# A two-layer decode and prefill step on one core: weight sums go along the mixer, norm-finishing products come later in TensorE's queue, GpSimd makes a part of the low parts at the token join

## The chip, the core and the metric

The kernel runs on one core of a Trainium2 chip. The metric is the device time of one execution, in microseconds (us), as the median of several. The engines are TensorE (PE in the rows; PEld is its weight load), VectorE (DVE), ScalarE (ACT), GpSimd (POOL) and SyncE (SP); SP issues most of the DMAs, GpSimd some. `SPq` and `POOLq` are what an engine's queue issues without computing.

## The reference, cut to what matters

Two layers run over 1,088 tokens (1,024 of a prompt, 64 of a sample: 8 sequences of 8). Layer 0 mixes by an RWKV-7 recurrence of 12 heads, layer 1 by latent attention of 6 heads over a shared latent (for the sample over a paged cache of 4,096 tokens); both add a memory attention. Behind each mixer come the output projection and a gated convolutional feed-forward block:

```python
x = x + jnp.concatenate([o_tok, o_mem], axis=-1) @ P['w_o'][l]           # 1024 x 1024
f, c = conv_glu(rms_norm(x, P['norm_ffn'][l]), conv0[l], P['w_ffn_up'][l],
                P['conv_w'][l], P['conv_b'][l], P['w_ffn_down'][l])
x = x + f
# conv_glu: u = xn @ w_up (1024 x 5632); gate, val = u[..., :2816], u[..., 2816:]
#           h = silu(conv3(gate)) * val;  return h @ w_down (2816 x 1024), ...
# rms_norm: x * rsqrt(mean(x * x) + eps) * gain
```

All is float32. An exact product of two float32 operands is made as three TensorE products of a high part and a low part (L481 to L483 and L1354 to L1356): `high` is the operand rounded by ScalarE (L210, L1137, L1313), `low` is operand minus high, a subtraction by VectorE or GpSimd (L211, L1138, L1314).

## The kernel before, in words

The tokens stand in two halves of 544, each of two quarters of 272. The stages follow one another in the trace: the mixer of layer 0 (up to 790 us its units, up to 940 us what ends it), the output projection of layer 0 (940 to 1130 us), its feed-forward block (to 1840 us), the start of layer 1 with the latents (to 1968 us), its prompt attention (1968 to about 2450 us), the decode over the paged cache (to about 2650 us), the output projection of layer 1 (to 2775 us), its feed-forward block and the final norm (to 3541 us).

**Weight sums.** The up-projection saves products: `combine_x` (L1214 on) makes seven combinations of a half's activations, and each 128 columns take seven combinations of the weights. Four of those are sums of blocks of `w_ffn_up`, called vg, gg, vgg and all, and `sum_weights(l)` (L1277 on) has them made in DRAM by DMAs alone, 32 per layer, 1,408 KB each, all on L1292. Sixteen are plain moves, issued by SP on the queue that also loads every weight tile. Sixteen are moves that add to what is there, issued by GpSimd. They come in the order: move vg, move gg, add vg, add gg, move vgg, add vgg, move all, add all, four row blocks `r` of each. A vgg or an all move waits for an add, and its add waits for that move; each is kept where the program puts it in its queue. `sum_weights` is a generator, and one `yield` is one DMA.

**Order of the work.** The order is written by hand: `merge` takes a list of generators with weights and steps them in proportion. The mixer has 12 units (6 head pairs by 2 halves), and `s.take(sums, 4)` lets each unit from the second on issue four steps of layer 0's sums; they are used up in the eighth. Layer 1's sums go two at a time into `prompt_attention`, one pair per iteration.

**Norm finishing.** The squares of a residual go through ScalarE (L1174) and are added up by GpSimd into `acc` (L1175). `scales` (L1203 on) then sums over the partitions by a TensorE product with a constant (L1209) and makes the reciprocal root by ScalarE (L1211, L1212). TensorE takes its instructions in order, so it stands at L1209 until GpSimd's last addition. In `trunk_tail`, `project(h)` ends with the `scales` of its half. `squares(0)` (L1177 on; L1187, L1188) makes the same for the first half behind the feed-forward block of layer 0, for the latents, in `down_last`.

**Join.** A feed-forward block runs five groups of columns for the first half, then five for the second: `ups` and `down` of the group before are merged. Where the halves join, `combine_x(1)` (VectorE L1224, GpSimd L1227 to L1230, 28 splits by ScalarE and VectorE at L1137 and L1138) runs beside `down(0, 4)`, whose weights are split too (L210, L211).

Of the kernel before, what the change touches and what calls it, by code (L numbers as in the profile page):

```python
# [9 lines left out]
F32 = mybir.dt.float32  # L10
# [4 lines left out]
ALU = mybir.AluOpType  # L15
# [71 lines left out]
HT = NT // 2  # L87
QT = NT // 4
G4 = [(QT * i, QT) for i in range(4)]
# [11 lines left out]
class Step:  # L101
# [171 lines left out]
    def mixer_a(s, od, qmd, kvd):  # L273
# [95 lines left out]
        mkv = s.memory_kv(kvd, 0, ("tp", "ch", "y"))  # L369
        sums = s.sum_weights(0)  # L370
        for i in range(nu):
            g = []
            if i == 1:
                for j in range(1, (len(s.prows) + 127) // 128):
                    s.load_params(j, [nc.sync])
            if i > 1:
                g.append((chain(units[i - 2]), s.PW[0] + s.PW[1] * units[i - 2][0], s.PW[2]))
            if i:
                u = units[i - 1]
                g.append((s.a_inner(u[1], u[0], ctx[u]), s.PW[3] + s.PW[4] * u[0], s.PW[5]))  # L380
            g.append((front(units[i]), 130 if units[i][1] else 220))
            if i == 0:
                g.append((mkv, 22))
            else:
                g.append((s.take(sums, 4), 4))
            s.merge(g)
# [747 lines left out]

    def split(s, hi, lo, x):
        nc = s.nc
        nc.scalar.copy(hi, x)  # L1137
        nc.vector.tensor_tensor(lo, x, hi.bitcast(F32), ALU.subtract)  # L1138

# [37 lines left out]
    def squares(s, h, acc):  # L1177

        nc = s.nc
        for d in range(KC):  # L1180
            for c0, a in acc.items():
                xv = s.x[:, d, c0:c0 + QT]
                if d == 0:
                    nc.scalar.activation(a, xv, AF.Square)
                else:
                    sq = s.st([128, QT], "nt", s.ntb)
                    nc.scalar.activation(sq, xv, AF.Square)  # L1187
                    nc.gpsimd.tensor_tensor(a, a, sq, ALU.add)  # L1188
            yield
        for c0 in acc:  # L1190
            s.scales((c0, QT), acc)

    def new_acc(s, h, tag="acc", n=HT):

        a = s.st([128, n], tag, 2 if tag == "acc" else 1)
        s.rstd[h] = s.t(s.xp, [128, HT], "rstd", 2)
        return {QT * (2 * h + i): a[:, QT * i:QT * i + QT] for i in range(2)}
# [16 lines left out]
    def combine_x(s, h, gain, xs):  # L1214


        nc = s.nc
        xs += [s.new_xq() for _ in range(7)]
        lo, hi = slice(0, QT), slice(QT, HT)
        for j in range(4):  # L1220
# [10 lines left out]
            src = (a[0][:, lo], t[1], t[0], t[2], t[3], a[1][:, hi], a[1][:, lo])  # L1231
            for (xh, xl), z in zip(xs, src):
                s.split(xh[:, j], xl[:, j], z)
                yield
# [81 lines left out]

    def ffn(s, l, xs0, after, pre=None):

# [95 lines left out]
        groups = [(0, 4), (4, 4), (8, 4), (12, 5), (17, 5)]  # L1414
        hs = {}
        operands = [xs0, []]

        def ups(h, i):
            c0, n = groups[i]
            hs[h, i] = []  # L1420
            if h and i == 0:
                yield from s.combine_x(1, ("norm_ffn", 8 * l), operands[1])
            for c in range(c0, c0 + n):
                yield from up(h, c, operands[h], hs[h, i])

# [6 lines left out]

        def down(h, i):
            yield from s.gemm_x(lambda d: wd(i, d), quarters(hs.pop((h, i))), h)

        def down_last():
# [25 lines left out]
            first = s.seq(*[after(g, None) for g in G4[:2]])  # L1462
            if l == 0:
                first = s.seq(s.squares(0, s.new_acc(0, "cv", EW)), first)
            return (yield from s.gemm_t(ws, hs.pop((1, i)), acc, after, [[first, s.conv_out(l, cout)], []]))
# [41 lines left out]
    def trunk_tail(s, l, od, xd, qmd, xst):  # L1507

        nc, I = s.nc, s.I
        with s.phase(f"f{l}", {"mm": 6, "dn": 2}):  # L1510
            s.xp = s.sp
            s.ntb, s.LAG, s.WA = 6, 2, 8
            xdv = xd.rearrange("(k p) t -> p k t", p=128)
# [6 lines left out]
            with s.sub(f"o{l}"):  # L1520
                first = [s.x_tile(i, nc.gpsimd) for i in range(2)] if l == 0 else []
                s.lay(([128, QT], "nt", s.ntb), ([128, HT], "tw", 2), ([128, HT], "acc", 2))
                os_ = []
# [28 lines left out]

                def project(h):
                    acc = s.new_acc(h)
                    yield from s.gemm_x(w, os_[h], h, acc, "mm")
                    for g in G4[2 * h:2 * h + 2]:
                        s.scales(g, acc)
                    yield

# [4 lines left out]
                if l == 0:  # L1564
                    s.drain(s.load_x(first))
                s.merge([(project(0), 17), (parts(os_[1]), 16)])
                s.merge([(project(1), 17), (s.combine_x(0, ("norm_ffn", 8 * l), xs), 32)])
            xl = {}

# [6 lines left out]
            with s.sub(f"n{l}"):  # L1576
                pend = s.emit(s.ffn(l, xs, stored if l == 0 else s.final, s.first_latent if l == 0 else None))
                if l:
                    s.drain(pend)
# [344 lines left out]
    def prompt_attention(s, od):  # L1924
        s.AT = (3, 2, 1, 2, 6, 3)
        s.HN = ((8, 12, 12, 1000), (8, 12, 14, 1000))
        with s.phase("pa", dict(zip(("sc", "tp", "o", "mm"), s.AT))):
# [7 lines left out]
            pr = None  # L1935
            sums = s.sum_weights(1)
            for i in range(len(us) + 1):
# [6 lines left out]
                if i < len(us):  # L1944
# [6 lines left out]
                    if pr is not None:  # L1951
                        k = s.HN[h % 2][Q]
                        g.append((s.take(pr, k), min(k, 40)))
                s.merge([(ao, n), (s.take(sums, 2), 2)] + g)

# [468 lines left out]
```

## Time and profile before

| | |
|---|---|
| median of 3 runs | 3540.04 us (3537.58 to 3558.76) |
| the profiled execution's own time | 3542.77 us |
| its span, first to last instruction | 3541.0 us |
| mean granted TensorE clock | 0.953 of full speed |
| PE busy | 3283.3 us, 93% |
| DVE, ACT, POOL busy | 2331.1, 1724.7, 811.9 us |

TensorE is busy for 93% of the span, so the reader looks for the stretches where it is not, or where its clock is low, and for what ended each wait. A wait row reads: engine, tile and line that waited, what came last, microseconds in total, how often, the longest. A timeline row has start, duration, engine, line, operation, tiles, and in brackets the idle time before it and what ended it.

### The profile page before, as it was taken

The numbers are of one execution on the slowest core, as the hardware profiler recorded it, in microseconds if no ns is written. First come the engines' busy times: TensorE is split into PE (matmuls) and PEld (weight loads), VectorE is DVE, ScalarE is ACT, GpSimd is POOL, SyncE is SP. The second block draws the span as 40 slices with busy tenths as digits, with TensorE's granted clock in tenths as the row PEclk, the third lists the DMA queues.
The fourth block names the chain that finished last, engine by engine and source line by source line (L and its number), as shares of the span: only waits on it lengthen the run. The fifth ranks groups of instructions, "written<-read, shape, count | busy, mean of one in ns | idle before, by whom it ended". The sixth has DMA issues, their size and how long they took to land. (4 is left out here: it accounts for less than half of the span.)

```text
span 3541.0 us, 68611 instructions
## 1 busy us (share of the span) xinstructions
PE 3283.3 (93%) x25782; PEld 2815.4 (80%) x25782; DVE 2331.1 (66%) x5353; ACT 1724.7 (49%) x3769; POOL 811.9 (23%) x1204
## 2 busy tenths in 40 slices
PE   7898899999878999999998977899999999999998
PEld 5565677775578999899998766745659999989998
DVE  5775667785536877877774465634446777787776
ACT  5554545554546545555555343433335645454444
POOL 4332233231013111322224001111103211132221
PEclk9998599998889999999999988999999999999999
DMA  6464444123244554364432589345423544545443
GB/s 195 125 144 119 102 132 93 37 55 91 58 161 121 148 147 135 113 183 144 143 114 83 159 240 212 114 158 171 140 72 119 166 135 138 147 127 147 135 142 111
DMA packets 608048, 466.90 MB, mean 132 GB/s; under 512 B 51546, under 2 KB 575598, under 8 KB 601060
## 3 DMA queue, kind: packets, MB, share of 16 engines
q1 hardware_dynamic: 583924, 359.80, 34.3%
q0 software_dynamic: 18848, 98.07, 10.9%
q10 hardware_dynamic: 4944, 4.65, 0.4%
q8 instruction: 202, 3.31, 0.4%
q14 instruction: 130, 1.06, 0.1%
HBM read 436.67 MB, written 118.03 MB: 157 GB/s over the span
## 5 line engine op out<-in xcount | busy, mean ns | idle before, releaser
L1354 PE MATMUL pmm<-xh,uh 128*128 128x272 f32 x2464 | 716.8, 291 | 5.1 <-ACT xh L1137 2.8
L1355 PE MATMUL pmm<-xl,uh 128*128 128x272 f32 x2464 | 714.0, 290 | 3.2 <-DVE xl L1138 2.9
L1356 PE MATMUL pmm<-xh,ul 128*128 128x272 f32 x2464 | 715.1, 291 | 0.4 <-DVE ul L1314 0.4
L1313 ACT CAST uh<-wa 128x512 fp32r<-128x512 f32 x610 | 378.3, 622 | 487.5 <-PE pmm L1355 308.8
L1314 DVE TENSOR_TENSOR ul<-wa,uh 128x512 fp32r<-128x512 f32 x610 | 435.4, 719 | 96.9 <-ACT uh L1313 52.6
L1354 PEld LDWEIGHTS pmm<-xh,uh 128*128 128x128 f32 x2464 | 466.9, 190 | 7.0 <-ACT xh L1137 4.3
L1355 PEld LDWEIGHTS pmm<-xl,uh 128*128 128x128 f32 x2464 | 467.6, 190 | 5.0 <-DVE xl L1138 4.5
L1356 PEld LDWEIGHTS pmm<-xh,ul 128*128 128x128 f32 x2464 | 466.5, 189 | 1.1 <-DVE ul L1314 0.9
L481 PE MATMUL pdn<-hh,wh 128*128 128x272 f32 x1248 | 360.9, 290 | 7.6 <-ACT hh L1137 3.9
L482 PE MATMUL pdn<-hl,wh 128*128 128x272 f32 x1248 | 358.4, 289 | 0.7 <-DVE hl L1138 0.7
L483 PE MATMUL pdn<-hh,wl 128*128 128x272 f32 x1248 | 357.2, 288 | 1.6 <-DVE wl L211 1.6
L210 ACT CAST wh<-wr 128x512 fp32r<-128x512 f32 (+2 forms) x363 | 200.5, 563 | 274.4 <-PE pdn L482 115.0
L1361 POOL TENSOR_TENSOR ext<-nt,nt 128x272 f32<-128x272 f32 (+2 forms) x132 | 119.1, 916 | 881.8 <-ACT uh L1313 710.8
L481 PEld LDWEIGHTS pdn<-hh,wh 128*128 128x128 f32 x1248 | 235.3, 189 | 12.9 <-ACT hh L1137 7.9
L483 PEld LDWEIGHTS pdn<-hh,wl 128*128 128x128 f32 x1248 | 235.0, 189 | 2.5 <-DVE wl L211 2.5
L482 PEld LDWEIGHTS pdn<-hl,wh 128*128 128x128 f32 x1248 | 235.3, 189 | 1.1 <-DVE hl L1138 1.1
L211 DVE TENSOR_TENSOR wl<-wr,wh 128x512 fp32r<-128x512 f32 (+2 forms) x271 | 166.6, 624 | 91.4 <-ACT wh L210 87.5
L1166 DVE TENSOR_TENSOR x<-x,pdn 128x272 f32<-128x272 f32 x288 | 125.5, 436 | 132.8 <-PE pdn L483 132.2
L481 PE MATMUL pmm<-xn,wh 128*128 128x292 f32 (+2 forms) x552 | 206.5, 374 | 2.6 <-DVE e L511 1.9
L482 PE MATMUL pmm<-xn,wh 128*128 128x292 f32 (+2 forms) x552 | 194.8, 353 | 0.0
L483 PE MATMUL pmm<-xn,wl 128*128 128x292 f32 (+2 forms) x552 | 194.4, 353 | 0.0
L211 POOL TENSOR_TENSOR wl<-wr,wh 128x512 fp32r<-128x512 f32 (+1 forms) x92 | 119.6, 1304 | 197.7 <-ACT wh L210 151.5
(760 smaller groups left out, 7820.1 us busy)
## 6 DMA issues: line engine op xcount, KB each, us to landing
wa<-in_w_ffn_up SPq DMA_DIRECT2D x262, 256.0 KB
wr<-in_w_ffn_down SPq DMA_DIRECT2D x164, 256.0 KB
wr<-in_w_in_a SPq DMA_DIRECT2D x84, 256.0 KB
wr<-in_w_o SPq DMA_DIRECT2D x64, 256.0 KB
wa<-ws0vg SPq DMA_DIRECT2D x44, 256.0 KB
wa<-ws0all SPq DMA_DIRECT2D x44, 256.0 KB
wa<-ws1vg SPq DMA_DIRECT2D x44, 256.0 KB
wa<-ws1all SPq DMA_DIRECT2D x44, 256.0 KB
```

The source lines that it names most:

```text
L210: nc.scalar.copy(wh[:, :n, :m], wr[:, :n, :m])
L211: s.wl_eng.tensor_tensor(wl[:, :n, :m], wr[:, :n, :m], wh[:, :n, :m].bitcast(F32), ALU.subtract)
L481: nc.tensor.matmul(ps[:m, :n], wh[:, :m], xh[:, c0:c0 + n], start=(k == 0), stop=False)
L482: nc.tensor.matmul(ps[:m, :n], wh[:, :m], xl[:, c0:c0 + n], start=False, stop=False)
L483: nc.tensor.matmul(ps[:m, :n], wl[:, :m], xh[:, c0:c0 + n], start=False, stop=(k == last))
L1166: nc.vector.tensor_tensor(xv, xv, p[:, :n], ALU.add)
L1313: nc.scalar.copy(wh, w)
L1314: nc.vector.tensor_tensor(wl, w, wh.bitcast(F32), ALU.subtract)
L1354: nc.tensor.matmul(p, wh, xh[:, k], start=k == 0, stop=False)
L1355: nc.tensor.matmul(p, wh, xl[:, k], start=False, stop=False)
L1356: nc.tensor.matmul(p, wl, xh[:, k], start=False, stop=k == 3)
L1361: add = lambda eng, o, a, b, op=ALU.add: eng.tensor_tensor(o, a, b, op)
```

## The change

First, one sequence of both layers' sums, `s.sums`, is taken five per unit in the mixer: 55 steps. The nine that are left (the last vgg add, the four moves and the four adds of "all", layer 1) go into the first half's output projection of layer 0. `prompt_attention` issues none. Second, the `scales` of the first half stand in `first_x`, four steps into the second half's projection, and `combine_x(0)` follows them; those of the second half are called by `ffn` before the second block of columns; `squares(0)` of layer 0 goes into the third column group of the second half and its `scales` into the fourth. The `acc` tiles change pools for it, and the up-weight buffers go from 8 to 7. Third, `split` takes an engine: at the join 3 of the 7 subtractions for each of four `j` go to GpSimd (12 per layer), and so do the weights' subtractions of `down(0, 4)` (eight 128x512 and eight 128x128 per layer).

```diff
-        sums = s.sum_weights(0)
+        s.sums = s.seq(s.sum_weights(0), s.sum_weights(1))
...
-                g.append((s.take(sums, 4), 4))
+                g.append((s.take(s.sums, 5), 5))
...
-    def split(s, hi, lo, x):
+    def split(s, hi, lo, x, eng=None):
         nc = s.nc
         nc.scalar.copy(hi, x)
-        nc.vector.tensor_tensor(lo, x, hi.bitcast(F32), ALU.subtract)
+        (eng or nc.vector).tensor_tensor(lo, x, hi.bitcast(F32), ALU.subtract)
...
-        for c0 in acc:
-            s.scales((c0, QT), acc)
-
-    def new_acc(s, h, tag="acc", n=HT):
+
+    def new_acc(s, h, tag="acc", n=HT, keep=False):
-        a = s.st([128, n], tag, 2 if tag == "acc" else 1)
+        a = s.t(s.up, [128, n], tag, 1) if keep else s.st([128, n], tag, 1)
...
-            for (xh, xl), z in zip(xs, src):
-                s.split(xh[:, j], xl[:, j], z)
+            for i, ((xh, xl), z) in enumerate(zip(xs, src)):
+                s.split(xh[:, j], xl[:, j], z, nc.gpsimd if h and i % 2 else nc.vector)
                 yield
...
             for c in range(c0, c0 + n):
+                if h == 0 and c == 1:
+                    normed()
+                if l == 0 and h and i == 2 and c == c0:
+                    acc0.update(s.new_acc(0, keep=True))
+                    yield from s.squares(0, acc0)
+                if l == 0 and h and i == 3 and c == c0:
+                    for g in G4[:2]:
+                        s.scales(g, acc0)
                 yield from up(h, c, operands[h], hs[h, i])
...
         def down(h, i):
+            s.wl_eng = nc.gpsimd if h == 0 and i == len(groups) - 1 else nc.vector
...
-            if l == 0:
-                first = s.seq(s.squares(0, s.new_acc(0, "cv", EW)), first)
...
-            s.ntb, s.LAG, s.WA = 6, 2, 8
+            s.ntb, s.LAG, s.WA = 6, 2, 7
...
-                def project(h):
-                    acc = s.new_acc(h)
-                    yield from s.gemm_x(w, os_[h], h, acc, "mm")
+                accs = [s.new_acc(h, keep=h == 1) for h in range(2)]
+
+                def normed(h):
                     for g in G4[2 * h:2 * h + 2]:
-                        s.scales(g, acc)
-                    yield
+                        s.scales(g, accs[h])
+
+                def first_x():
+                    for _ in range(4):
+                        yield
+                    normed(0)
+                    yield from s.combine_x(0, ("norm_ffn", 8 * l), xs)
...
-                s.merge([(project(0), 17), (parts(os_[1]), 16)])
-                s.merge([(project(1), 17), (s.combine_x(0, ("norm_ffn", 8 * l), xs), 32)])
+                s.merge([(s.gemm_x(w, os_[0], 0, accs[0], "mm"), 16), (parts(os_[1]), 16)] + ([(s.sums, 9)] if l == 0 else []))
+                s.merge([(s.gemm_x(w, os_[1], 1, accs[1], "mm"), 16), (first_x(), 36)])
...
-                pend = s.emit(s.ffn(l, xs, stored if l == 0 else s.final, s.first_latent if l == 0 else None))
+                pend = s.emit(s.ffn(l, xs, lambda: normed(1), stored if l == 0 else s.final, s.first_latent if l == 0 else None))
...
-            sums = s.sum_weights(1)
...
-                s.merge([(ao, n), (s.take(sums, 2), 2)] + g)
+                s.merge([(ao, n)] + g)
```

SP's queue where the output projection of layer 0 begins, before (`xt` are token tiles, `wr` weight tiles; the changed program's lines stand a few off from the profile's):

```order
L1144 DMA xt_2251_11390<-in_x_prompt 128x1024
L207 DMA wr_2271_11560<-in_w_o 128x4x128
L1144 DMA xt_2254_11404<-in_x_prompt 128x1024
L207 DMA wr_2278_11628<-in_w_o 128x4x128
L1144 DMA xt_2257_11418<-in_x_sample 64x1024
L207 DMA wr_2281_11634<-in_w_o 128x4x128
L207 DMA wr_2288_11702<-in_w_o 128x4x128
```

Only tiles that the stage itself uses stand there.

The same place on SP in the change:

```order
L1144 DMA xt_2259_11421<-in_x_prompt 128x1024
L207 DMA wr_2277_11592<-in_w_o 128x4x128
L1144 DMA xt_2262_11435<-in_x_prompt 128x1024
L1290 DMA ws1all_1080_5307<-ws1vgg_1079_5306 32x11264
L1144 DMA xt_2265_11449<-in_x_sample 64x1024
L1290 DMA ws1all_1080_5307<-ws1vgg_1079_5306 32x11264 x2
L207 DMA wr_2284_11661<-in_w_o 128x4x128
L207 DMA wr_2287_11667<-in_w_o 128x4x128
L1290 DMA ws1all_1080_5307<-ws1vgg_1079_5306 32x11264
```

Four moves of the sums now stand among the last token tiles and the first weights of the projection.

GpSimd's queue in the first half's projection, in the change (`acc` are the sums of squares; before, the L1175 rows follow one another with nothing between):

```order
L1290 DMA ws1vgg_5306<-in_w_ffn_up 128x2x1408
L1175 TENSOR_TENSOR acc_11278<-acc_11278,nt_11549 128x272
...
L1175 TENSOR_TENSOR acc_11278<-acc_11278,nt_11774 128x272
L1290 DMA ws1all_5307<-in_w_ffn_up 128x2x1408
L1175 TENSOR_TENSOR acc_11278<-acc_11278,nt_11881 128x272
L1175 TENSOR_TENSOR acc_11278<-acc_11278,nt_11924 128x272
L1290 DMA ws1all_5307<-in_w_ffn_up 128x2x1408
L1175 TENSOR_TENSOR acc_11278<-acc_11278,nt_11956 128x272
L1175 TENSOR_TENSOR acc_11278<-acc_11278,nt_11999 128x272
L1290 DMA ws1all_5307<-in_w_ffn_up 128x2x1408
```

Adds of the sums stand between the additions of squares, one add to two of them.

GpSimd's queue at the join of layer 0, in the change (L1225 to L1228 are L1227 to L1230 of before, where they alone stand here, four times):

```order
L1225 TENSOR_TENSOR nt_17520<-tw_17516 128x272
L211 TENSOR_TENSOR wl_17634<-wr_17631,wh_17633 128x512
L211 TENSOR_TENSOR wl_17640<-wr_17637,wh_17639 128x128
L1226 TENSOR_TENSOR nt_17521<-tw_17518,nt_17520 128x272
L1227 TENSOR_TENSOR nt_17522<-tw_17516,tw_17518 128x272
L1228 TENSOR_TENSOR nt_17523<-tw_17518,nt_17521 128x272
L1138 TENSOR_TENSOR xl_17505<-nt_17521,xh_17504 128x272
L1225 TENSOR_TENSOR nt_17592<-tw_17588 128x272
L1138 TENSOR_TENSOR xl_17509<-nt_17522,xh_17508 128x272
L1138 TENSOR_TENSOR xl_17513<-tw_17518,xh_17512 128x272
L211 TENSOR_TENSOR wl_17706<-wr_17703,wh_17705 128x512
```

The low parts `xl` and `wl` now stand between the combinations `nt` that they are made from.

## Rows read from the trace of the kernel before

**Rows 1.** The page: busy time, share of the span and instructions per engine.

```profile
PE 3283.3 (93%) x25782; PEld 2815.4 (80%) x25782; DVE 2331.1 (66%) x5353; ACT 1724.7 (49%) x3769; POOL 811.9 (23%) x1204
```

**Rows 2.** Windows: stretch, its length, busy time by engine, granted clock, DMA share, GB/s.

```profile
200.00:400.00 200.00, 175.14 (x1614) 112.12 (x1614) 134.48 (x419) 100.86 (x244) 59.47 (x81) 0.81 0.60 143
600.00:790.00 190.00, 184.40 (x1952) 137.38 (x1951) 146.99 (x437) 101.86 (x251) 62.47 (x99) 0.99 0.17 44
1024.00:1080.00 56.00, 54.07 (x426) 53.69 (x425) 20.46 (x36) 23.95 (x41) 12.82 (x16) 1.00 0.26 76
1080.00:1130.00 50.00, 43.83 (x334) 43.16 (x334) 38.69 (x67) 29.12 (x65) 24.94 (x29) 0.96 0.32 95
1470.00:1510.00 40.00, 33.67 (x231) 30.78 (x229) 36.51 (x66) 20.99 (x49) 20.30 (x26) 0.96 0.23 66
1968.00:2200.00 232.00, 187.11 (x1154) 161.26 (x1153) 128.09 (x351) 89.45 (x236) 21.66 (x30) 0.90 0.84 218
2200.00:2450.00 250.00, 222.35 (x1362) 143.81 (x1363) 110.73 (x312) 90.30 (x257) 33.91 (x36) 0.93 0.44 143
2450.00:2650.00 200.00, 197.41 (x1370) 119.48 (x1370) 92.85 (x240) 77.70 (x234) 27.80 (x30) 1.00 0.34 119
```

**Rows 3.** Waits of ScalarE, 1968 to 2250 us: total, times, longest.

```profile
ACT wh L210 <- DMA wr<-in_w_o: 18.2, 1, 18.2
ACT wh L210 <- DMA wr<-in_w_q_b: 17.3, 2, 16.4
ACT wh L210 <- DMA wr<-in_w_kv_b: 13.5, 2, 12.2
```

**Rows 4.** Waits of TensorE, 1968 to 2250 us.

```profile
PE psc L1865 <- ACT P L1883: 23.1, 6, 15.9
PE pmm L481 <- ACT ql L1823: 15.2, 1, 15.2
PE po L1915 <- ACT ptH L1137: 11.7, 4, 10.8
```

**Rows 5.** Line L1292, the sums: operation, tile, count, duration in ns, first and last start.

```profile
L1292 POOL DMA_DIRECT2D ws0all<-in_w_ffn_up x4: 1181/1190/1204, 508.4 to 570.4; - x4
...
L1292 POOL DMA_DIRECT2D ws1gg<-in_w_ffn_up x4: 1584/2283/2979, 2079.0 to 2081.1; - x4
...
  DMA ws1vgg<-ws1vg: 43.5, 1
```

**Rows 6.** Waits in the mixer, 0 to 790 us, ScalarE.

```profile
ACT wh L210 <- DMA wr<-in_w_in_a: 14.7, 3, 12.0
```

**Rows 7.** Waits in the mixer, 0 to 790 us, TensorE.

```profile
PE pch L917 <- ACT r L913: 11.2, 4, 10.4
```

**Rows 8.** Timeline of SyncE in the first half's projection of layer 0.

```profile
1026.72 44.30 SPq L207 DMA_DIRECT2D wr<-in_w_o  x16
```

**Rows 9.** Timeline of ScalarE, the same stretch: a high part of weights.

```profile
1031.40 0.62 ACT L210 CAST wh<-wr 128x512 fp32r<-128x512 f32 x1 [0.48 <-PE pmm L482]
```

**Rows 10.** Waits of TensorE over the whole span.

```profile
PE pmm L1156 <- DMA xt<-in_x_prompt: 18.2, 4, 6.4
...
PE pdn L1209 <- POOL acc L1175: 15.2, 4, 5.8
...
PE pdn L1209 <- POOL cv L1188: 8.8, 1, 8.8
```

**Rows 11.** Timeline of GpSimd at the join of layer 0.

```profile
1485.07 1.61 POOL L1227 TENSOR_TENSOR nt<-tw 128x272 f32<-128x272 f32 x1 [2.83 <-DVE tw L1224]
...
1491.77 0.77 POOL L1227 TENSOR_TENSOR nt<-tw 128x272 f32<-128x272 f32 x1 [2.40 <-DVE tw L1224]
```

**Rows 12.** Lines by form, 1474 to 1510 us: busy, mean ns, idle before.

```profile
L1138 DVE TENSOR_TENSOR xl<-nt,xh 128x272 fp32r<-128x272 f32 x16 | 10.2, 672 | 1.8 <-ACT xh L1137 1.8
...
L211 DVE TENSOR_TENSOR wl<-wr,wh 128x512 fp32r<-128x512 f32 x4 | 3.2, 809 | 0.0
```

**Rows 13.** Lines by form, GpSimd, whole span.

```profile
L211 POOL TENSOR_TENSOR wl<-wr,wh 128x512 fp32r<-128x512 f32 x88 | 117.5, 1339 | 190.7 <-ACT wh L210 144.5 <-PE pmm L483 10.3 <-issue 8.8
```

More of the change, by code (lines that the diff above doesn't have):

```diff
@@ L1315, in load_up, with ffn @@
             yield [(wh[:, k], wl[:, k]) for k in range(4)]
-    def ffn(s, l, xs0, after, pre=None):
+    def ffn(s, l, xs0, normed, after, pre=None):
         nc, I = s.nc, s.I
@@ L1414, in ffn @@
         groups = [(0, 4), (4, 4), (8, 4), (12, 5), (17, 5)]
-        hs = {}
+        hs, acc0 = {}, {}
         operands = [xs0, []]
@@ L1521, in trunk_tail @@
                 first = [s.x_tile(i, nc.gpsimd) for i in range(2)] if l == 0 else []
-                s.lay(([128, QT], "nt", s.ntb), ([128, HT], "tw", 2), ([128, HT], "acc", 2))
+                s.lay(([128, QT], "nt", s.ntb), ([128, HT], "tw", 2), ([128, HT], "acc", 1))
                 os_ = []
```

## The prediction, as it was put on record before the changed kernel was run

> **What bounds the kernel now.** The page comes first: TensorE is busy for 3283.3 of 3541.0 us [rows 1], so 258 us of idle time and the stretches at a low clock are all there is to win, short of fewer products, and the change leaves the products alone. The windows say where that time is [rows 2]. The feed-forward blocks are nearly full and are left out. Prompt attention is not: in 1968 to 2200 us TensorE is busy 187.1 of 232 us at a clock of 0.90 of full speed, and the DMA engines 0.84; in the decode, 2450 to 2650 us, it is busy 197.4 of 200 at 1.00, with DMA at 0.34. ScalarE's waits name what comes late in between: weight tiles, for 18.2, 16.4 and 12.2 us at the longest [rows 3]. Three waits of TensorE answer to them: 15.9, 15.2 and 10.8 us [rows 4], together 42 us. Layer 1's sums are issued there; the four adds of gg start within 2.1 us [rows 5]. Sixteen adds and sixteen moves lift the DMA share by 0.84 - 0.34 = 0.50 of 232 us, so one of the 32 takes an estimated 3.6 us of all DMA engines.
>
> In the mixer layer 0's 32 went by at far less cost: the weights came late for 14.7 us in all on ScalarE, once for 12.0 [rows 6], and TensorE's answer is at most the 10.4 us of [rows 7]. That is 0.33 us of TensorE per DMA of the sums, against 42 / 32 = 1.3 in attention. Attention loads a weight tile now and then, and its next product needs it; the mixer has other heads' products between.
>
> Then the small ones: TensorE waits for GpSimd's sum of squares at the projections' ends, 15.2 us in four waits, and 8.8 us once behind layer 0's feed-forward block [rows 10]. At the join of the halves it is idle for 40 - 33.7 = 6.3 us, and there VectorE is the fullest, 36.5 of 40 us [rows 2].
>
> **The change part by part.**
>
> *Sums out of attention.* The 42 us go. The clock: an average of 0.90 over 232 us between the levels 1.2 and 2.4 GHz is 46 us at the lower one. Most of these lie in the waits themselves, where nothing is lost; if all were busy, 23 us would be. I take 8, and 50 for this part; ends 35 (a third of the waits is put down to transfers that come late anyway, such as attention's own tiles) and 65.
>
> *Sums into the mixer.* 55 steps in place of 32, so 23 more, five per unit where there were four, from the second unit to the last. Nothing shows this density. From below the mixer's own price: 23 x 0.33 = 7.5 us; below nothing there is no reason to go, since no wait is removed. From above attention's price, clock included, on all 55: 50 / 32 = 1.56 us, 55 x 1.56 - 10.4 = 75 us. DMA is at 0.60 in 200 to 400 us, but at 0.17 in 600 to 790 us [rows 2], where most of the added steps fall, so I take a value near the lower end, 18 us. An add waits for its move in GpSimd's queue (43.5 us in attention at the longest [rows 5]); behind it stand the mixer's masks and decay products, but the adds come four yields or more behind their moves, about a unit later, so no such wait is in the sum.
>
> *The last nine into the first half's projection.* TensorE is busy there for 54.1 of 56 us [rows 2] and takes weights steadily: 16 loads in 44.3 us [rows 8], each cast waiting for a product, not for its load [rows 9]. Four moves stand ahead of the first ones on the same queue and four adds run beside the later ones. Lower end nothing; upper end two waits like attention's longest, 36 us; at 1.3 us a step 12 us. It is a stretch without slack, so I take 16 us. The token tiles ahead of it already wait for DMA, 18.2 us in four waits [rows 10], and the vgg add beside them can only lengthen that; this lies within the 16.
>
> *Scales later.* Of the 15.2 us, the first half's waits go entirely, since another 6 us of products precede the L1209 pair; the second half's are covered by 12 groups of three products at 0.13 us each, 4.7 of their 5.8 us. What is late next is `combine_x(0)`: it starts some 7 us later and has VectorE busy for 38.7 of the 50 us [rows 2], with 36 steps to the projection's 16 in place of 32 to 17. It may end 0 to 5 us after the projection, in each layer. So 12 us gained, ends 0 and 20. The moved `squares(0)` frees 8 of the 8.8 us, with ends 0 and 13; its 14 additions and two table loads in mid-block are covered, because TensorE there waits for neither engine.
>
> *Join.* VectorE loses 12 subtractions of 0.67 us and eight of 0.81 us [rows 12], 14 us. GpSimd, busy for 20.3 of 40 us [rows 2], gains 12 at 1 us or so and eight at 1.34 us [rows 13] and eight small ones, an estimated 12 + 11 + 3 = 26 us: 46 in a window of 40. The join can win its 6 us or lose as much. I take nothing, with ends of 11 us won and 8 lost per layer.
>
> The Trainium skill speaks against this part: in "SBUF — State Buffer", section "Who interferes with whom", a VectorE instruction with two SBUF inputs and a GpSimd instruction that reads SBUF exclude each other for their whole length. The trace agrees as far as it goes: the same L1227 took 0.77 us and 1.61 us within one join [rows 11]. By that rule the two engines' work at the join adds up, which is the rival "join" below.
>
> *Up-weight buffers, 8 to 7.* One buffer less of prefetch costs nothing while the feed-forward windows are full; 0 to 5 us.
>
> **The sum**, against the profiled execution's own 3542.8 us: -50 + 18 + 16 - 12 - 8 + 0 = -36, so 3506.8 us. The median of the runs stands 2.7 us below that execution: **3504 us**.
>
> **The rivals.**
>
> *The sums are hidden altogether.* The mixer's second half has its DMA engines idle for four fifths, and the weights of the projection arrive early enough. Then 18 + 16 becomes 7.5 + 5, and the clock gives another 5: 3504 - 27 = 3477 us. For it: 0.33 us per step; against it: five per unit, and the full TensorE of the projection. 0.22.
>
> *The sums hold up the mixer and the projection as they held up attention* (slower). Place: weight tiles queued on SP while adds run. It decides when adds come in clusters of four, as in attention [rows 5]. A wait for a move makes clusters, since the adds behind it are then issued at once. Price: 75 us in the mixer, 36 in the projection, so 111 - 34 = 77 more than in the sum: 3581 us; halfway, 3542. It decides from an average of 0.8 us per step on, where the mixer's 55 x 0.8 - 10.4 = 34 and the projection's 36 eat up the 50 + 20 that are gained. The Trainium skill describes such a mechanism in "DMA: Bandwidth & Descriptors", section "Queues, rings and completion order": each DMA engine takes turns between its queues, a packet at a time. By that, a weight load advances by its small packets only between an add's large ones, wherever the add is put; attention's 12 to 18 us for one tile [rows 3] agree, the mixer's single 12.0 us [rows 6] shows it rarely matters there. 0.17, of which half ends slower than before by over 1%.
>
> *The join.* GpSimd becomes the bound: 46 us of work in 40, +6 per layer, or, if its reads hold VectorE's subtractions too, 46 + 36.5 - 14 = 68.5, of which perhaps 61 cannot overlap, +21 per layer: 12 to 42 us, so 3516 to 3546 us. Against it: the page has GpSimd at 23%, and the low parts come far ahead of their products. 0.13.
>
> The forecast keeps 0.48. Of the range, 3477 less a few for the hidden case and the upper ends of the mixer and the join hold 8 in 10: 3470 to 3548 us. About 1% (35 us, 3504.6 and 3575.4) is what can be told from no change here. The forecast is half below it: 0.24, and the hidden case 0.22: faster 0.46. Slower by over 1% needs nearly the full price of the second rival: 0.09. The rest, 0.45, is within 1%.
>
> **What would show it.** In the profile after: attention's window without the waits on `in_w_o`, `in_w_q_b` and `in_w_kv_b` and with a DMA share near 0.5; the waits of L1209 below 5 us in all; ScalarE's waits for `wr<-in_w_in_a` in the mixer at 15 to 40 us, and for `wr<-in_w_o` in the projection at 10 to 20; the join's idle time between 3 and 10 us. The forecast is wrong if attention keeps its waits under other names (its tiles late for another reason), if units of the mixer stretch by more than 3 us each, or if GpSimd ends last at the join.

## The result and the profile after

The change made the kernel slower by 0.84% (ratio 1.0084, interval 1.0059 to 1.0109): 3569.43 us against 3537.58 us, medians of 11 runs each. The prediction said 3504 us, 3470 to 3548; the time lies above the range, and the sign is the other one.

The profiled execution took 3580.78 us, 11 us more than the median. Its page:

```profile
PE 3324.8 (93%) x25782; PEld 2844.2 (79%) x25782; DVE 2325.6 (65%) x5297; ACT 1728.1 (48%) x3770; POOL 865.8 (24%) x1260
```

As many products as before [rows 1] keep TensorE busy for 41.5 us more. The windows tell where, if each stage is cut at the same product in both programs. Windows of before (stretch, length, busy time and instructions of PE, PEld, DVE, ACT, POOL, granted clock, DMA share, GB/s): mixer units, what follows them (left out here), last token tiles and transposes, projection, the two halves of layer 0's feed-forward block, start of layer 1, prompt attention.

```profile
0.00:802.00 802.00, 725.16 (x6592) 521.15 (x6592) 568.43 (x1692) 419.03 (x987) 264.67 (x395) 0.92 0.43 112
...
957.00:1018.00 61.00, 33.76 (x136) 25.67 (x136) 20.80 (x48) 29.07 (x66) 9.46 (x13) 0.64 0.62 212
1018.00:1128.00 110.00, 101.90 (x779) 100.84 (x777) 61.80 (x111) 54.40 (x114) 37.45 (x43) 0.97 0.27 80
1128.00:1477.00 349.00, 346.61 (x2719) 344.46 (x2717) 263.14 (x461) 182.50 (x319) 60.41 (x92) 0.99 0.52 149
1477.00:1851.00 374.00, 367.05 (x2876) 363.56 (x2875) 289.99 (x540) 188.17 (x350) 97.34 (x166) 1.00 0.48 139
1851.00:2014.00 163.00, 150.46 (x1065) 138.86 (x1063) 77.58 (x164) 79.28 (x160) 42.44 (x58) 0.97 0.35 111
2014.00:2302.00 288.00, 225.41 (x1358) 192.00 (x1358) 167.36 (x491) 118.99 (x332) 31.52 (x36) 0.87 0.73 189
```

The same stages in the changed kernel:

```profile
0.00:859.00 859.00, 760.68 (x6593) 543.95 (x6594) 566.22 (x1692) 419.73 (x986) 274.86 (x406) 0.87 0.55 143
...
1023.00:1093.00 70.00, 35.25 (x139) 26.36 (x138) 24.04 (x57) 32.34 (x75) 10.66 (x14) 0.62 0.74 250
1093.00:1216.00 123.00, 105.39 (x772) 103.82 (x773) 56.67 (x95) 47.62 (x97) 40.87 (x45) 0.92 0.53 134
1216.00:1573.00 357.00, 347.04 (x2717) 343.86 (x2717) 266.37 (x463) 184.79 (x325) 67.15 (x99) 0.98 0.51 147
1573.00:1964.00 391.00, 373.49 (x2886) 370.39 (x2885) 288.82 (x517) 202.86 (x376) 130.04 (x205) 0.97 0.46 133
1964.00:2112.00 148.00, 146.36 (x1058) 136.14 (x1056) 76.73 (x164) 68.81 (x137) 30.76 (x42) 1.00 0.27 83
2112.00:2331.00 219.00, 209.32 (x1359) 179.38 (x1359) 166.37 (x491) 118.81 (x331) 13.43 (x20) 1.00 0.19 65
```

Attention gives back 69 us, and the start of layer 1 another 15. The mixer's units take 57, what follows them up to the transposes 9, the transposes 9, the projection 13, the two halves of the block 8 and 17, layer 1's block with the end 12, and the rest gives 3. That is the 38 us of the spans. In the mixer idle time grew by 21.5 us (98.3 against 76.8) and busy time by 35.5 us for the same 6,593 products (but one): the clock fell from 0.92 to 0.87. By these two averages TensorE stood at the lower of its two levels (1.2 and 2.4 GHz) for an estimated 128 of 802 us before and 223 of 859 us after. More than half of the mixer's loss is therefore no wait at all. In attention it is the other way round: of the 69 us that come back, 53 are idle time (62.6 against 9.7) and 16 are busy time at the higher clock.

Waits of TensorE over the whole span, after (tile and line that waited, what came last, us in total, times, longest):

```profile
PE pch L917 <- ACT r L913: 27.0, 10, 14.1
...
PE pmm L481 <- ACT wh L210: 17.4, 4, 7.4
PE pdn L481 <- DVE x L1166: 15.4, 11, 2.6
...
PE pdn L1333 <- DMA wa<-in_state_conv: 9.0, 2, 5.5
PE pdn L481 <- ACT hh L1137: 8.4, 17, 5.0
PE pmm L1353 <- ACT uh L1311: 6.4, 2, 3.2
```

And ScalarE's for weights, the mixer's and the projections' (29.1 of the 31.4 us are in layer 0's projection):

```profile
ACT wh L210 <- DMA wr<-in_w_in_a: 40.8, 8, 14.5
...
ACT wh L210 <- DMA wr<-in_w_o: 31.4, 6, 12.4
```

The waits of L1209 [rows 10] are gone, all 24 us. In their place stand the first columns of the blocks (L1333 for the convolution state, 9.0 us, where before had none; L1353 for the first up-weights, 6.4 us, where before had 2.1) and, in mid-block, two waits that the timeline of the second half shows:

```profile
1733.33 0.82 PE L481 MATMUL pdn<-hh,wh 128*128 128x272 f32 x2 [4.96 <-ACT hh L1137]
```

```profile
1805.86 0.59 PE L481 MATMUL pdn<-hh,wh 128*128 128x272 f32 x1 [2.40 <-ACT rstd L1209]
```

The first stands behind ScalarE's squares, the second behind the root of the `scales`, whose partition sum holds one of the two `pdn` buffers that the down-projection also needs.

### The profile page after: what moved, and what is told of

Read it like the earlier page. It is cut to its first block, busy times and chain, and to the rows that moved or that the text cites. A ratio compares the mean times of both kernels' runs of the same rounds, so it can differ in the third digit from the quotient of the medians.

```text
span 3579.0 us, 68648 instructions
## 1 busy us (share of the span) xinstructions
PE 3324.8 (93%) x25782; PEld 2844.2 (79%) x25782; DVE 2325.6 (65%) x5297; ACT 1728.1 (48%) x3770; POOL 865.8 (24%) x1260
## 3 DMA queue, kind: packets, MB, share of 16 engines
q0 software_dynamic: 18848, 98.07, 10.8%
## 5 line engine op out<-in xcount | busy, mean ns | idle before, releaser
L1353 PE MATMUL pmm<-xh,uh 128*128 128x272 f32 x2464 | 713.7, 290 | 6.4 <-ACT uh L1311 6.4
L1353 PEld LDWEIGHTS pmm<-xh,uh 128*128 128x128 f32 x2464 | 465.7, 189 | 6.7 <-ACT uh L1311 6.6
L481 PE MATMUL pdn<-hh,wh 128*128 128x272 f32 x1248 | 366.0, 294 | 26.3 <-DVE x L1166 15.4
L481 PEld LDWEIGHTS pdn<-hh,wh 128*128 128x128 f32 x1248 | 239.2, 192 | 33.2 <-ACT hh L1137 12.2
L481 PE MATMUL pmm<-xn,wh 128*128 128x292 f32 (+2 forms) x552 | 208.6, 378 | 5.5 <-DVE e L508 3.6
L211 POOL TENSOR_TENSOR wl<-wr,wh 128x512 fp32r<-128x512 f32 (+1 forms) x124 | 150.5, 1221 | 231.8 <-ACT wh L210 197.7
L211 DVE TENSOR_TENSOR wl<-wr,wh 128x512 fp32r<-128x512 f32 (+2 forms) x239 | 151.8, 641 | 68.3 <-ACT wh L210 64.6
```

The lines of the kernel that those rows point to most:

```text
L211: s.wl_eng.tensor_tensor(wl[:, :n, :m], wr[:, :n, :m], wh[:, :n, :m].bitcast(F32), ALU.subtract)
L481: nc.tensor.matmul(ps[:m, :n], wh[:, :m], xh[:, c0:c0 + n], start=(k == 0), stop=False)
L1353: nc.tensor.matmul(p, wh, xh[:, k], start=k == 0, stop=False)
```

## The experiments

Ratios are against before on the same chip, whose median was 3551.72 us for the first four kernels, 3540.86, 3548.13 and 3543.15 for the later ones.

**sums_only**: before with the sums' move alone (the diff's first two and last two changes, and the nine steps in the projection).

> The kernel before with the move of the sums alone (five per unit, the last nine in the projection, none in attention). Theory: the sums take from the mixer and the projection about what they give back in attention, mostly through the clock: mixer +45 to +60 us, projection +12 to +20, attention -60 to -70, so 3535 to 3555 us. Rival (the join on GpSimd makes the change slow, the sums pay as predicted): 3500 to 3515 us.

3546.87 us, ratio 0.9979 (0.9956 to 1.0001). The move pays almost nothing: attention took 228 us in place of 288, and the units of the mixer 861 in place of 802. The rival's 3500 to 3515 is out.

**sums_back**: the change with both layers' sums where they were.

> The change with the sums where they were before; norms, join and 7 buffers as in the change. Theory: the latents gain about 14 us, the two joins lose about 14 together, the starts of the feed-forward blocks nothing: 3530 to 3548 us, with TensorE's clock in the mixer as before. Rival (the clock's loss in the mixer is chance of an execution and not of the sums): a loss of 20 us or more of half-clock time beyond before in this run's mixer too.

3573.74 us, ratio 1.0069 (1.0041 to 1.0096), 22 us slower, where I expected 3530 to 3548 (on a chip 14 us slower than the first). Norms and join cost more than the latents' 15 us bring. The mixer took 813 us at 0.91; other profiles with before's order of work in the mixer lie between 802 and 813 us. So about 10 us of mixer time can be scatter, and the sums explain the rest of the change's 57.

**l1_out**: layer 1's sums left out; its block takes layer 0's.

```diff
-        s.sums = s.seq(s.sum_weights(0), s.sum_weights(1))
+        s.sums = s.sum_weights(0)
+        s.wsum[1] = s.wsum[0]        # in trunk_tail
...                                   # and no steps in the projection
```

> The change without layer 1's sums: its feed-forward block takes layer 0's sums in their place, so 32 DMAs of the sums are left out. Theory: this gives the price of these 32 DMAs in mixer and projection, 60 to 80 us: 3490 to 3510 us, with about 100 us at the lower clock before 800 us as in the kernel before. Rival (layer 0's sums, now five per unit, do the harm): above 3540 us.

3539.81 us, ratio 0.9974 (0.9953 to 0.9995): about 0.3% under before, against 0.84% over it with these DMAs, so they cost 1.1%, some 39 us, less than the 60 to 80 us of the theory; that price holds the other order of work that comes with them. The mixer was at 826 us and 0.90: layer 0's sums alone, at five per unit in place of four, keep some of the loss.

**join_back**: the low parts of the join on VectorE again.

```diff
-                s.split(xh[:, j], xl[:, j], z, nc.gpsimd if h and i % 2 else nc.vector)
+                s.split(xh[:, j], xl[:, j], z, nc.vector)
-            s.wl_eng = nc.gpsimd if h == 0 and i == len(groups) - 1 else nc.vector
+            s.wl_eng = nc.vector
```

> The change with all low parts of the join on VectorE again. Theory: 6 to 10 us per layer come back, 3550 to 3558 us, and the waits of L481 on the residual at the join go. Rival (GpSimd's part is neutral and the move of products is what costs at the join): within 4 us of the change.

3569.70 us, ratio 1.006 (1.0036 to 1.0083). The interval overlaps that of the change; the trace is sharper. The second halves of the two blocks, windows of join_back:

```profile
1560.00:1946.00 386.00, 372.10 (x2879) 368.37 (x2879) 292.35 (x541) 201.89 (x375) 107.27 (x180) 0.98 0.46 135
3141.00:3514.00 373.00, 366.05 (x2880) 362.50 (x2880) 289.59 (x537) 186.00 (x341) 98.62 (x167) 1.00 0.47 135
```

The change has 391 us for the first and 380 for the second: 5 and 7 us come back, and L481's wait for the residual (a VectorE addition) falls from 15.4 us to 3.7. What stays in layer 0, 386 against 374, goes with the moved squares: norms_only below, which has them without the sums, takes 382. VectorE's own instructions tell why it gained so little. At layer 0's join, the change from 1573 to 1625 us (line, tile, shape, count, busy us, mean ns, idle before):

```profile
L1222 DVE SCALAR_TENSOR_TENSOR tw<-x,ptile,rstd 128x544 f32<-128x544 f32 x7 | 8.6, 1226 | 3.8 <-POOL nt L1227 3.8
L1138 DVE TENSOR_TENSOR xl<-tw,xh 128x272 fp32r<-128x272 f32 x7 | 6.8, 980 | 0.3 <-ACT xh L1137 0.3
```

join_back, the same stretch, 1560 to 1612 us:

```profile
L1222 DVE SCALAR_TENSOR_TENSOR tw<-x,ptile,rstd 128x544 f32<-128x544 f32 x7 | 5.7, 838 | 0.0
L1138 DVE TENSOR_TENSOR xl<-tw,xh 128x272 fp32r<-128x272 f32 x11 | 5.7, 521 | 0.0
```

With GpSimd busy for 34.4 of the first 40 us of the join in place of 17.1, the instructions that VectorE kept became longer, the same seven `tw` by 2.9 us in all. Layer 1's join shows the same (1230 against 836 ns).

**tiny**: sums_only with layer 1's DMAs cut to one row in 128; its block takes layer 0's sums.

```diff
+                m = 1 if l else 128
-                ...dma_start(out=S[z][r:r + 128], in_=src[r:r + 128], **kw)
+                ...dma_start(out=S[z][r:r + m], in_=src[r:r + m], **kw)
```

> The kernel of sums_only with every DMA of layer 1's sums cut to one of its 128 rows, at the same places in every queue; layer 1's block takes layer 0's sums. TensorE's order is that of sums_only product by product. Theory (bytes): late weights and through them the clock cost the mixer 45 us, so they go with the bytes: mixer units as before, 3480 to 3505 us. Rival (order): the sums' steps shift the order of TensorE's products in the mixer, and that order has the low clock whatever the bytes: unit 8 to 9 again some 105 us in place of 75, about 150 to 190 us busy at the lower clock before 860 us, 3520 to 3540 us.

3515.93 us, ratio 0.9918 (0.9892 to 0.9945), between the two forecasts. The mixer's loss stayed although layer 1's bytes went; what went with them are 15 us of the mixer's idle time (83.1 against 98.6 in sums_only) and the losses behind it. **four** is the counterpart: all bytes, four steps per unit.

```diff
-                g.append((s.take(s.sums, 5), 5))
+                g.append((s.take(s.sums, 4), 4))
```

> The kernel of sums_only with four steps per unit of the mixer as before, 44 in place of 55, the other 20 in the projection of layer 0. TensorE's order in the mixer is that of before up to about unit 7 and then another one. Theory (the order of products sets the mixer's time, not the bytes): units up to 7 as before within 5 us, though after that the result is open (a third order); projection 15 to 40 us longer. Rival (the number of DMAs in units 9 to 12 makes the loss): unit 8 to 11 loses 25 to 40 us here too, since 12 more DMAs stand there than before.

3583.23 us, ratio 1.0100 (1.0057 to 1.0143): the twenty steps cost the projection 69 us, more than the 15 to 40 expected (ScalarE waited 87.8 us for `in_w_o` there). To its last product it took, against the 110 us of before:

```profile
1047.00:1226.00 179.00, 113.75 (x769) 110.92 (x769) 61.29 (x102) 49.55 (x106) 48.11 (x52) 0.80 0.73 187
```

But the mixer's units, in the windows of sums_only, tiny and four (four has 72 products of 16 columns and a few others behind the cut):

```profile
0.00:861.00 861.00, 762.42 (x6594) 544.44 (x6594) 566.72 (x1692) 419.14 (x986) 274.77 (x406) 0.87 0.55 143
```

```profile
0.00:854.00 854.00, 770.91 (x6593) 549.92 (x6594) 567.42 (x1692) 418.79 (x986) 270.31 (x406) 0.87 0.41 106
```

```profile
0.00:806.00 806.00, 726.64 (x6515) 520.86 (x6516) 566.15 (x1690) 419.15 (x986) 269.15 (x399) 0.92 0.51 133
```

With DMA at 0.41 the mixer takes 854 us, with DMA at 0.51 it takes 806; up to the transposes four loses another 12 us. Bytes do not make the loss of the units. What tiny shares with sums_only, and four does not, is five steps per unit and with them the sequence in TensorE's queue: they shift how the large products of the next heads' projections (L481, 292 columns) stand among the small ones of the recurrence. Counted in the traces (a product by source line, tiles and shape, equal ones in a row as one), of some 3,390 rows ahead of the token transposes about 2,220 stand in the same sequence in sums_only and in before, about 2,920 in four and in before; sums_only and tiny are alike but for a row or two. The windows of L481 alone (PE busy, count, clock, DMA share, GB/s) show what goes with the clock. Before, at the ninth unit:

```profile
605.00:625.00 20.00, 3.88 (x11) 1.00 0.23 54
625.00:645.00 20.00, 7.82 (x23) 1.00 0.10 29
```

The change, at the same unit and a little later:

```profile
615.00:635.00 20.00, 2.79 (x6) 0.50 0.44 86
635.00:655.00 20.00, 5.26 (x9) 0.50 0.16 35
655.00:675.00 20.00, 8.41 (x25) 0.99 0.42 88
675.00:695.00 20.00, 1.64 (x5) 0.69 1.05 215
```

tiny, at the same unit:

```profile
620.00:640.00 20.00, 2.90 (x8) 0.79 0.18 50
640.00:660.00 20.00, 3.58 (x8) 0.70 0.19 41
660.00:680.00 20.00, 7.60 (x22) 1.00 0.15 42
```

In these rows the windows at the lower level, 1.2 GHz, are among those with few of the large products. It is no rule: four, with nine of them, stayed at 2.4 GHz:

```profile
605.00:625.00 20.00, 3.30 (x9) 1.00 0.45 138
```

Before had a stretch at the lower level too, with none of them:

```profile
370.00:390.00 20.00, 0.00 (x0) 0.50 0.97 183
```

In the change TensorE is shown busy all through the first of the two low stretches, 615 to 655 us (windows of all engines):

```profile
620.00:640.00 20.00, 20.00 (x110) 11.33 (x111) 5.12 (x13) 4.65 (x12) 3.39 (x5) 0.50 0.57 112
```

The Trainium skill, in "TensorE: Matmul & The Clock Gate", section "HAM oscillation — how this bites in real kernels", puts a falling clock down to waits for DMA between bursts of products. That fits attention before, where waits and low clock went together and left together. It fits the change's second low stretch as well, 683 to 714 us, which begins with the 14.1 us wait of L917 shown above, at a DMA share of 1.05. It does not fit the first stretch, which has no wait; here the measurement decides.

**late55** and **five40** put the same 55 steps elsewhere in the units.

```diff
+                k = 4 if i < 9 else 8 if i < 11 else 7
-                g.append((s.take(s.sums, 5), 5))
+                g.append((s.take(s.sums, k), k))          # late55
+                g.append((s.take(s.sums, 5), 40))         # five40
```

> The kernel of sums_only with the same 55 steps in the mixer, but four per unit up to the eighth and eight, eight and seven per unit after that; the last nine in the projection. TensorE's order is that of before up to unit 7. Theory (the mixer's time follows the order of its products, not the number or the bytes of the DMAs): within 15 us of before at the mixer's end although eight full DMAs stand in a unit, total 3490 to 3510 us. Rival (more than four DMAs of the sums in a unit cost, by issue time or bytes): the last units lose 40 us or more, total at 3540 or above.

> The kernel of sums_only with weight 40 in place of 5 for the sums in each unit's merge, so that the five steps stand at the unit's beginning: same count, same bytes, another order of TensorE's products. Theory (order): the loss of 60 us at the mixer's end changes by 15 us or more in either direction. Rival (five per unit): it stays within 10 us.

late55: 3547.80 us, ratio 1.0020 (1.0002 to 1.0039); the theory's 3490 to 3510 us failed, and what the rival forecast came: its units with four steps kept step with before (596 us against 591 at the ninth), those with eight lost 50 us. five40: 3588.42 us, ratio 1.0125 (1.0102 to 1.0149). Their mixers:

```profile
0.00:856.00 856.00, 754.54 (x6514) 539.02 (x6514) 564.34 (x1689) 418.54 (x982) 277.80 (x406) 0.87 0.56 143
```

```profile
0.00:919.00 919.00, 800.39 (x6594) 567.48 (x6594) 568.78 (x1692) 421.76 (x988) 274.73 (x406) 0.82 0.51 134
```

Five steps per unit cost 60 or 117 us by where they stand in the unit, with the same count and bytes. So neither sets the price by itself; the clock (0.92 in four, 0.87 in sums_only, tiny and late55, 0.82 in five40) follows the mixer's time. Held issues do not set it either: in five40, the slowest, GpSimd waited for none of its moves and SP 3.4 us for an add, against 13.7 and 8.6 us in the change. That it is the sequence of products alone is likely but not shown. Every kernel with more than four steps in a unit lost time, and no kernel changed the sequence without the steps. And weights came later too: ScalarE waited for `in_w_in_a` for 14.7 us before, 19.2 in four, 21.6 in tiny, 33.9 in late55, 42.1 in sums_only and 69.0 in five40. In tiny late weights are half of those in sums_only and the mixer is 7 us shorter; in five40 they can be a larger part.

**fused**: 32 steps that each carry both layers' blocks (2,816 KB, half a row's columns each).

> Before's 32 steps in the mixer, but each DMA carries both layers' blocks (2,816 KB), so all sums are made there with no more DMAs than before, and attention has none. TensorE's order in the mixer is yet another one. Theory (order, not bytes): mixer between 0 and 50 us longer as the order falls out, with waits for weights below 30 us; attention gains 60. Rival (bytes): weights late by 60 us or more in the mixer, more than in sums_only, and a total above before.

5403.44 us, ratio 1.522 (1.517 to 1.527). This tells nothing of order: in this form there were 75,936 packets on GpSimd's queue in place of 18,848, and ScalarE waited 613 us for weights.

**norms_only** and **norms_early**: before with the norm products and seven buffers; then one step in place of four ahead of the first half's `scales`.

```diff
-                    for _ in range(4):
+                    for _ in range(1):
```

> The kernel before with the later norm products and seven buffers alone. Theory: latents -14, squares in mid-block +12, each projection with the start of its block +4 to +7 us, so 8 to 14 us slower than before. Rival (the scales are covered and only the join costs): 5 to 15 us faster than before.

> The kernel of norms_only with one step in place of four ahead of the first half's scales, so that combine_x starts earlier. Theory: the start of the block waits because VectorE, late with combine_x, splits weights late and so keeps SP from loading; then the waits for state_conv (5.5 us) and for the first up-weights (3.2 us) shrink by half or more, 4 to 8 us faster than norms_only. Rival (seven buffers make those waits): no difference.

3546.05 us, ratio 1.0020 (1.0000 to 1.0039), and 3547.38 us, ratio 1.0023 (1.0008 to 1.0037). The norms gain nothing, and an earlier `combine_x` does not help: the theory of a late VectorE fell. norms_only's rows:

```profile
PE pdn L481 <- ACT hh L1137: 8.4, 17, 5.0
PE pdn L1333 <- DMA wa<-in_state_conv: 8.1, 2, 4.3
PE pmm L1353 <- ACT uh L1311: 6.4, 2, 3.2
PE pdn L481 <- ACT rstd L1209: 2.4, 1, 2.4
```

**seven**: before with seven up-weight buffers.

```diff
-            s.ntb, s.LAG, s.WA = 6, 2, 8
+            s.ntb, s.LAG, s.WA = 6, 2, 7
```

> The kernel before with 7 up-weight buffers in place of 8, nothing else. Theory (the start of a block waits because its tiles come free only at the projection's end, and the wait for the scales used to cover it): no wait for state_conv above 1 us, time within 4 us of before. Rival (seven buffers make the start wait): 4 to 8 us per layer lost, slower by 8 to 16 us.

3546.43 us, ratio 0.9995 (0.9977 to 1.0013): the buffers are not it, and its start of a block shows no wait for the state. In before SP issued the state's loads at 1129.2 us, 7.8 us after the projection's last product began, and in norms_only at 1137.5 us, 5.5 us after it. Such a gap stands in both; the wait of 5.6 us at L1209 used to cover it. What holds the loads until then, tiles of the projection that come free late, was not tried by itself.

**ffn_sums**, **ffn_spread** and **mix44** look for a better place.

```diff
+        sums = s.sum_weights(1) if l == 0 else iter(())      # in ffn
-                s.merge([(down(*order[n - 1]), 16), (s.take(u, 64), 64)])
+                s.merge([(down(*order[n - 1]), 16), (s.take(u, 64), 64), (s.take(sums, 4), 4)])   # ffn_sums
                 yield from up(h, c, operands[h], hs[h, i])
+                if h or i:
+                    next(sums, None)                         # ffn_spread, without the take
...                                                          # attention issues none
```

> The kernel before with layer 1's sums moved from attention into layer 0's feed-forward block, four per pair of column groups; norms, join and mixer as before. Theory: attention gives 55 to 65 us, the block loses 0 to 20 us, 3490 to 3505 us on a chip where before takes 3551. Rival (an add delays weights wherever the weights are needed, 1.3 us per step): 42 us lost in the block, about 3530 us.

> The kernel of ffn_sums with one step of layer 1's sums behind each block of columns, so that no four steps come close together. Theory: the block loses half or less of the 20 us that ffn_sums lost, 10 us faster than ffn_sums, 1.5% faster than before. Rival (each step costs the same wherever it stands): no difference to ffn_sums.

> Before with the sums in sequence, four per unit in the mixer (44 steps), and the 20 that are left one behind every second block of columns of layer 0's feed-forward block; norms and join as before. Theory: mixer as in four, 0 to 5 us over before, the block loses 5 to 12 us, attention gives 60: 45 to 55 us below before, as good as ffn_spread or better. Rival (20 adds and moves cost the block 1 us each, as in ffn_sums): 40 us below before.

ffn_sums: 3498.34 us, ratio 0.9880 (0.9849 to 0.9910). ffn_spread: 3500.68 us, ratio 0.9874 (0.9834 to 0.9915). mix44: 3501.08 us, ratio 0.9885 (0.9859 to 0.9911). All three beat before by 1.1 to 1.3% (intervals 0.8 to 1.7%), and they cannot be told apart; the 10 us that spreading the steps was to add do not show. ffn_spread's block and attention:

```profile
1136.00:1497.00 361.00, 349.12 (x2717) 346.81 (x2717) 262.24 (x461) 181.13 (x319) 68.03 (x100) 0.98 0.80 219
1497.00:1870.00 373.00, 367.09 (x2876) 363.89 (x2875) 289.61 (x539) 187.31 (x349) 106.91 (x174) 0.99 0.71 190
2029.00:2256.00 227.00, 212.77 (x1363) 181.93 (x1362) 166.64 (x491) 119.30 (x332) 13.44 (x20) 0.98 0.18 62
```

Full adds beside a TensorE at 97% cost 12 us in the first half of the block and nothing in the second, at a DMA share of 0.71 to 0.80; attention gives 61 us. TensorE's sequence in the mixer is that of before in ffn_spread. mix44 left the units as in four, but lost some 20 us between the last unit and the transposes.

## Why the prediction was wrong, point by point

Between the sum's -36 us and the +38 us of the two profiled executions lie 74. The mixer's units give 39 of them (57 us where 18 were priced) and what follows them 9; the feed-forward blocks, where norms and join were to give 12 and took 37, 49; the transposes and the projection 6. Attention, the start of layer 1 and the rest took 29 back. So two steps failed: the price of the added steps in the mixer, and the gain of the later norms with a free join.

- **Sums out of attention, -50 (ends 35 and 65).** Right in kind, too small: -60 us in sums_only and in ffn_spread, -69 in the change's own profile. Waits gave 53 of the 69 us, where 42 were priced, and the clock 16, where 8 were (0.87 to 1.00).
- **Sums into the mixer, +18 (ends 7.5 and 75).** This step failed. I priced 23 DMAs by how late they make weights, and the weights did come late, 40.8 us on ScalarE in place of 14.7 [rows 6]; TensorE felt 21.5 us of it at most. The other 35.5 us is the lower clock for the same products, which the 18 us leave out; only the upper end carries attention's clock, and as a price of late weights. The measured 57 us lie within the ends, near the upper one, and the units grew by the more than 3 us each that were named as a sign of being wrong. "Nothing shows this density" was treated as a question of traffic, while tiny and four show that traffic decides little. A third of TensorE's sequence in the mixer changes, and the queues compared ahead of the prediction are those of SP and GpSimd only. The wait of an add for its move, put at nothing, came once, 13.7 us on GpSimd.
- **The last nine in the projection, +16.** About right: 14 us in sums_only with the transposes (67 and 118 us against 61 and 110). In the change the two took 22 us more, and ScalarE's waits for `in_w_o` there were 29 us, not 10 to 20.
- **Scales later, -12.** Failed: 15.2 us of waits went and 13.3 us came (L1333 9.0, L1353 4.3 more). I named `combine_x` as what is late next; it was the first loads of the block.
- **Squares, -8.** The gain was there, 15 us at the start of layer 1. "TensorE there waits for neither engine" was false: 5.0 and 2.4 us of waits, and 12 us in all in the second half (join_back: 386 against 374).
- **Join, 0.** 5 and 7 us lost, within the ends (8 lost per layer) and 12 us in all, the rival's lower price. Its mechanism was not GpSimd as the bound: TensorE waited there for VectorE's residual (8.0 us in layer 0) and little for GpSimd (1.4 us). That the two engines exclude each other is seen in part: VectorE's `tw` took 1226 ns in place of 838. For all of GpSimd's work it would have given 42 us, which did not come.
- **Seven buffers, 0.** Right (seven).
- **The rivals.** The second rival had the side right, the place in part, and the mechanism wrong: 3569 lies between its halfway 3542 and its full 3581, but with late weights as the smaller share; that the total falls between its two prices is luck. I gave it 0.17, mostly because the mixer's own price per step was low. That price held again at four steps per unit (four: 806 us against 802 with 12 more steps) and not at five.

The parts do not add up: sums_only is at -0.2%, norms_only at +0.2%, the join by its trace at 12 us or +0.3%, together 0.3%, and the change at +0.84%. Of the some 18 us that are left over, the projection shows about 8 (123 us in the change, 118 in sums_only, 107 in norms_only, 110 before) and the first half of layer 0's block 3 or so (357, against 354 in norms_only). The rest lies within the intervals of about 0.2% either way, and its cause stays open.

## What to carry to other kernels

When a change adds instructions to a list that is scheduled together with others, compare the sequence on the engine that bounds, over the whole stretch, before pricing the added instructions: their issue may cost little and the reshuffle that comes with them 50 us. A TensorE shown as busy is not one at the full clock (620 to 640 us here: busy for 20.00 of 20 us at 0.50), so read the granted clock of a stretch beside its busy time. And when a wait is taken away, look at what was loaded under its cover.

## What the runs showed of the hardware

- A DMA of the sums (1,408 KB; half of them plain moves, half adds) beside a matrix stage cost about 0.4 us per step (12 us for 32 steps) in the feed-forward block, 1.9 us in attention (60 us for 32) and 3.5 us in the projection (69 us for 20): the price of the same transfer differed by the stage it stood in.
- With the sums' DMAs shaped as 2x256 rows of half the columns, GpSimd's queue had four times the packets (75,936 against 18,848), and the kernel took 5403 us.
- VectorE's `tw` (128x544) at the join took 1226 ns on average beside a GpSimd busy for 34.4 of 40 us, and 838 ns beside one busy for 17.1.
- The clock in the mixer differed by 0.10 (0.92 in before, 0.82 in five40) between programs with the same products.
